# A mixture-of-experts kernel: activation, extra rows and steps of a round rearranged

## The chip, the core and the metric

One NeuronCore of a Trainium2 chip runs the whole block: input layer norm, one projection, two kinds of mixers, output projection, router, 32 experts with four chosen for each token, and the last layer norm. The metric is the device time of one execution in microseconds. TensorE does matmuls into PSUM, VectorE and ScalarE work on PSUM and SBUF, POOL (GpSimd) issues the indirect DMAs that gather and scatter token rows, and SyncE's queue (SP) issues the loads of the weights.

## The reference, cut to what matters

1024 tokens of width 1024; each goes to 4 of 32 experts, with a gate for each. The change lies in the expert part and behind it:

```python
hid = xb @ w1[e] + b1[e]                                  # 128 rows x 2048
x_glu = jnp.minimum(hid[..., ::2], 7.0)
x_lin = jnp.clip(hid[..., 1::2], -7.0, 7.0)
act = x_glu * jax.nn.sigmoid(1.702 * x_glu) * (x_lin + 1)
out = act @ w2[e] + b2[e]                                 # times the gate, summed over each token's experts
h = layer_norm(DEEPNORM_ALPHA * h + ffn)                  # the last layer norm
```

## The kernel before

**Rounds.** The experts are worked off in 32 rounds. Round r does `up` of expert r (8 blocks, k = 0 to 7, of 128 rows of w1) and then `down` of expert r-1 (4 blocks, b = 0 to 3, of w2). Each block of weights is 128x2048 float32, 1 MB. `weights` (L1174) loads it as `raw` (SyncE, a ring of RB = 6 buffers), has ScalarE round it to `wh` (L1185) and VectorE take the rest `wl` (L1188); these two are issued three blocks ahead (AH). TensorE then multiplies three times, wh by the high part of the operand, wl by the high part, wh by the low part: 12 matmuls of 512 columns for a block (L1213 in `up`, L1271 in `down`).

**Extra rows.** An expert takes 128 tokens, and the 18 fullest take 32 more (NH = 18, CX = 32). The 32 extra rows are multiplied in plain float32 with `raw`, in four column groups of TensorE beside each other, one group for each 512 columns: `extra` in `up` (L1206) and in `down` (L1261). Before, `extra` was called for two blocks at a time (XB = 2), behind the blocks 1, 3, 5 and 7 of `up` and 1 and 3 of `down`. A `raw` buffer is free once ScalarE, VectorE and, with extra rows, `extra` have read it.

**Steps.** Behind each block the loop calls `step(s)`, s = 0 to 7 for `up` and 8 to 11 for `down`, and this issues whatever `plan` has put there. So the order on every engine is fixed by these numbers:
- MP = 6: `begin2(r+2)`, the mark `oh` of which token goes to which slot (VectorE, L1139).
- SLP = -4, that is step 8 of the round before: `third`, which calls `slots`: TensorE turns the mark into token numbers (L1014, for extra rows also L1020), VectorE copies them (`st` L1029, `sv` L1004), computes the index, and POOL gathers the rows `xg`. For extra rows one step later (SLE): L1026, a small transposition, and another gather, `xe`.
- XP: the gathered rows are transposed (`front`), two pieces of `xg` at steps 4 and 5 and `xe` (L1165) at step 7.
- DP = 8 and 9: the two halves of the activation (`swiglu`, L1222); the extra rows' part runs directly behind `up`.
- TP: the activation is transposed, two pieces (L1150, then `ah` on ScalarE and `al` on VectorE, L1153) at steps 11 and 13 (step 1 of the next round), and that of the extra rows (L1248) at 14 (step 2).

All transpositions and slots share one bank of PSUM, tag `tr`: each waits until VectorE and ScalarE have read the one before. `up` writes four banks (`h`), `down` two (`o`), the extra rows one (`ex`).

**The end.** Behind round 31 two transpositions of the last expert's mark go into `kept`, the tokens' sums `ya_d` are loaded again into four ring buffers (`sums`, L1410), and `down` of the last expert leaves its result in SBUF. A loop over overflow blocks (L1417) makes no pass with these inputs. Then `final_norm` adds the last expert's rows by a matmul with the mark, and normalises eight tiles in groups of 3, 3 and 2 (FG): statistics on VectorE, and for each group a chain of small VectorE operations for the inverse root (`chain`). `advance` issues one step of the chain at each call; when the chain is done `finish` scales on ScalarE, adds on POOL and stores.

The parts ahead of the experts are ordered by the framework's scheduler, the experts and the final norm by hand (`manual_schedule`).

Of the kernel before, what the change touches and what calls it, by code (L numbers as in the profile page):

```python
# [8 lines left out]
FT = mybir.dt.float32  # L9
# [9 lines left out]
P = 128  # L19
# [24 lines left out]
FIRST = 10  # L44
XP = (4, 5, 7)
TP = (11, 13, 14)
SLP = -4
SLE = 1
# [5 lines left out]

XB = 2
FG = (0, 3, 6, 8)
# [10 lines left out]
SWI = 1.702  # L67
LIMIT = 7.0


# [730 lines left out]
def post_mix(tc, A, L):  # L801
# [60 lines left out]
    def half():  # L862
        for t in range(NT):
            n = slice(t * P, (t + 1) * P)
            y = p3.tile([P, 512], FT, name="y", tag="h1", bufs=H1B)
            sp.dma_start(y, y_d[n, 0:512])
            h = p3.tile([P, D], FT, name="h", bufs=UB)
            sp.dma_start(h, h_d[n, :])
            m = turn(lambda j: y[:, j * P:(j + 1) * P])
            for c in range(2):  # L870
                q, ps = product(*m, wa, c)
                ve.scalar_tensor_tensor(h[:, q], h[:, q], ALPHA, ps, op0=OP.mult, op1=OP.add)
            sp.dma_start(u_d[n, :], h)
        L["wb"] = [load_wo(4 + k) for k in range(4)]
        for nm, src, sh in (("lw", bcast(A["ln1_w"], D), [P, D]), ("lb", bcast(A["ln1_b"], D), [P, D]),
                            ("rb", bcast(A["router_b"], NE), [P, NE])):
            L[nm] = p3.tile(sh, FT, name="p3" + nm)
            sp.dma_start(L[nm], src)

        raw = p3.tile([96, D], FT, name="b2r", tag="wor", bufs=2)  # L880
        for i in range(3):
            sp.dma_start(raw[32 * i:32 * i + 32], A["b2"])
        L["b2"] = p3.tile([96, D], FR, name="b2s")
        ac.copy(L["b2"], raw)
        ve.tensor_tensor(L["b2"][64:96], raw[64:96], f32(L["b2"])[64:96], op=OP.subtract)

        bh = L["bh"]
        for i in range(2):
            q = slice(i * FF, (i + 1) * FF)
            b1 = p3.tile([96, FF], FT, name="b1", tag="wor", bufs=2)  # L890
            for g in range(3):
                sp.dma_start(b1[32 * g:32 * g + 32], A["b1"][:, q])
            ac.copy(bh[:, q], b1)
            for n in (64, 32):
                ve.tensor_tensor(b1[:n], b1[:n], bh[:n, q], op=OP.subtract)
                ac.copy(bh[:n, q], b1[:n])
        L["rwt"] = p3.tile([P, KD + 3, NE], FT, name="rwt")
        gp.memset(L["rwt"][:, KD:], 0.0)
        sp.dma_start(L["rwt"][:, :KD], A["router_w"])
# [214 lines left out]
def experts(tc, A, L):  # L1114
# [3 lines left out]
    with ExitStack() as cx:  # L1118
# [54 lines left out]

        def weights(j, ahead):  # L1174

            while len(raws) < min(j + src[1], len(stream)):
                raw = wr.tile([P, 2 * FF], FT, name="raw", tag=src[0], bufs=src[2])
                sp.dma_start(raw, stream[len(raws)]())
                raws.append(raw)
            while len(ready) < min(j + 1 + ahead, len(stream)):  # L1180
                i = len(ready)
# [10 lines left out]
        def up(j0, sel, xh, xl, xt, step=lambda s: None):  # L1192
# [5 lines left out]

            def extra(k, raw):
                if px is None:  # L1200
                    return
                if k == 0:
# [4 lines left out]

            late = []
            for k in range(KD):
                raw, h, l = weights(j0 + k, AH[xt is not None] if src[0] == "raw" else 0)  # L1210
                for x, w, z in ((xh, h, False), (xh, l, False), (xl, h, k == KD - 1)):
                    for c, m in enumerate(cols):
                        pe.matmul(ps[:, c], x[:, k], w[:, m], start=False, stop=z)  # L1213
                late.append((k, raw))
                if len(late) == XB:
                    for b in late:
                        extra(*b)
                    late.clear()
                step(k)
            return ps, px  # L1220

        def swiglu(glu, lin, g, l, sg):  # L1222
            ve.tensor_scalar(g, glu, LIMIT, None, op0=OP.min)  # L1223
            ac.activation(sg, g, AF.Sigmoid, scale=SWI)  # L1224
            ve.tensor_scalar(l, lin, LIMIT, -LIMIT, op0=OP.min, op1=OP.max)
            ve.scalar_tensor_tensor(l, l, 1.0, g, op0=OP.add, op1=OP.mult)
            ve.tensor_tensor(l, l, sg, op=OP.mult)

# [23 lines left out]
        def down(j0, ah, al, ax, gate, idx, step=lambda s: None, o=None):  # L1252
            po = pq.tile([P, 2, 512], FT, name="o")
            px = pq.tile([P, 512], FT, name="ex") if ax is not None else None

            def extra(b, raw):
                for c in range(2 if px is not None else 0):
                    for kk in range(2):
# [3 lines left out]

            late = []
            for b in range(4):
                raw, h, l = weights(j0 + b, AH[ax is not None] if src[0] == "raw" else 0)
                for kk in range(2):
                    k = 2 * b + kk
                    for x, w, z in ((ah, h, False), (ah, l, False), (al, h, k == KD - 1)):
                        for c in range(2):
                            m = slice(1024 * kk + 512 * c, 1024 * kk + 512 * c + 512)  # L1270
                            pe.matmul(po[:, c], x[:, k], w[:, m], start=(k == 0 and x is ah and w is h), stop=z)  # L1271
                late.append((b, raw))
                if len(late) == XB:
                    for x in late:
                        extra(*x)
                    late.clear()
                step(KD + b)
# [58 lines left out]
        def step(r, s):  # L1336
            for f in jobs.pop(12 * r + s, ()):
                f()

        at = {}  # L1340
        for r in range(NE + 1):
# [6 lines left out]
        with tc.manual_schedule():  # L1348
# [11 lines left out]
            for r in range(NE):  # L1360
# [17 lines left out]
                parts, turns, a = act(*hid)  # L1378
                run_all(parts[:-2])
                for i in range(2):  # L1380
                    jobs.setdefault(12 * r + DP + i, []).insert(0, parts[i - 2])
                for w, f in zip(TP, turns):
                    plan(r, w, f)
# [8 lines left out]
            for s in range(KD):  # L1392
                step(NE, s)

            ring = lambda: wr.tile([P, 2 * FF], FT, name="raw", bufs=RB)
            kept = ring()
            oht = kept[:, :S].rearrange("p (t q) -> p t q", t=NT)
            for g in range(2):
                ps = pq.tile([P, 4, P], FT, name="tr")
                for j in range(4):  # L1400
                    pe.matmul(ps[:, j], last_oh[0][:, 4 * g + j], idb, start=True, stop=True)
                ac.copy(oht[:, 4 * g:4 * g + 4], ps)
            wb = ring().rearrange("p (i d) -> p i d", i=2)
# [4 lines left out]
            def sums():  # L1408
                for g, y in enumerate(ys):
                    sp.dma_start(y, ya_d[2 * g * P:2 * (g + 1) * P, :].rearrange("(t p) d -> p t d", p=P))  # L1410
            sums()
            down(at["d", NE - 1], *prev, o=kept[:, S:])
            pq_.__exit__(None, None, None)
# [36 lines left out]
def final_norm(tc, A, L, ep, pt, wb, ys, oht, o):  # L1450
# [50 lines left out]

    def advance(to_end=False):
        nonlocal run
        while run is not None:
            if next(run[0], run) is run:
                finish(*run[1:])
                run = None
            if not to_end:
                return

    for g0, g1 in zip(FG, FG[1:]):
        for t in range(g0, g1):
# [7 lines left out]
            advance()  # L1520
        advance(True)
        run = (chain(g0, g1), g0, g1)
        next(run[0])
    bp.append(pt.tile([P, 2, 512], FT, name="y", bufs=3))
    for c in range(2):
        pe.matmul(bp[0][:, c], L["ons"][0:1], wb[0:1, 1, 512 * c:512 * c + 512], start=True, stop=True)
    advance(True)

# [57 lines left out]
```

## Time and profile before

| what | value |
|---|---|
| median of 3 runs | 2582.07 us (2574.61 to 2583.59) |
| profiled execution | 2580.89 us, span 2579.2 us, granted TensorE clock 0.972 |
| TensorE (PE) busy | 2399.2 us, 93% |
| VectorE (DVE) busy | 1928.0 us, 75% |
| ScalarE (ACT) busy | 1321.3 us, 51% |
| POOL busy | 400.6 us, 16% |
| moved by DMA | 606.63 MB, mean 235 GB/s |

The shares are means over the whole span. The first 40% of it are the mixers and the router; the rounds of the experts begin at about 1035 us and the final norm at 2531.76 us. A group of instructions is named by the line of the kernel, the engine and the tiles (out<-in). A timeline row merges equal instructions that follow each other (x4 is four), and its duration reaches to the end of the last, which overlaps the start of the next group: the distance of two starts is what a group costs TensorE. In brackets is the idle time ahead of it and what ended it. PEclk is the granted clock as a share of full speed.

### The profile page before, as it was taken

Reading aid. Unit: us, or ns where it says so; the run is one execution under the profiler, and the core shown is the slowest. Engines: PE = TensorE matmul, PEld = TensorE weight load, DVE = VectorE, ACT = ScalarE, POOL = GpSimd, SP = SyncE. Lnnn points to the kernel's source line nnn. Section 1 sums busy time; section 2 is a strip of 40 time slices with the busy share of each in tenths; the row PEclk is TensorE's granted clock in tenths of the full one; section 3 lists DMA queues with packets and bytes.
Section 4 is the critical chain, followed back from the end, with each engine's and each line's share of the span. In section 5 each row is a group of like instructions: output and inputs, shape, how many; then the busy total and the mean of one; then the engine's idle time right before and its main releaser. Section 6 shows DMA issues by size and latency. Waiting matters only on the chain. (4 is left out here: it accounts for less than half of the span.)

```text
span 2579.2 us, 37473 instructions
## 1 busy us (share of the span) xinstructions
PE 2399.2 (93%) x14105; PEld 1808.3 (70%) x14105; DVE 1928.0 (75%) x2886; ACT 1321.3 (51%) x1610; POOL 400.6 (16%) x370
## 2 busy tenths in 40 slices
PE   5999998989988996899999999999999999999986
PEld 5778998977776674657666666766676666667663
DVE  8367334376887687779788888888888888888884
ACT  3254432354344432456666656666565655666661
POOL 4400211123122011011101011011110110111012
PEclk9999999999999997899999999999999999999998
DMA  6323864228446424768878778888877897788973
GB/s 228 130 74 136 284 203 86 69 70 259 158 150 242 138 83 180 258 206 308 299 301 322 274 294 301 311 292 322 297 282 284 312 330 282 277 298 306 344 279 136
DMA packets 184442, 606.63 MB, mean 235 GB/s; under 512 B 69881, under 2 KB 95609, under 8 KB 130626
## 3 DMA queue, kind: packets, MB, share of 16 engines
q1 hardware_dynamic: 155810, 525.24, 55.0%
q0 software_dynamic: 17456, 65.02, 8.9%
q10 hardware_dynamic: 10992, 13.93, 1.8%
q8 instruction: 113, 1.85, 0.3%
q14 instruction: 71, 0.58, 0.1%
HBM read 518.64 MB, written 85.50 MB: 234 GB/s over the span
## 5 line engine op out<-in xcount | busy, mean ns | idle before, releaser
L1188 DVE TENSOR_TENSOR wl<-raw,wh 128x2048 fp32r<-128x2048 f32 x384 | 873.8, 2289 | 195.2 <-ACT wh L1185 194.1
L1185 ACT CAST wh<-raw 128x2048 fp32r<-128x2048 f32 x381 | 720.6, 1906 | 110.6 <-DMA raw<-w 83.4
L1213 PE MATMUL h<-wh,xh 128*128 128x512 f32 x1024 | 299.6, 414 | 0.9 <-ACT wh L1185 0.9
L1213 PE MATMUL h<-wl,xh 128*128 128x512 f32 x1024 | 281.3, 396 | 1.1 <-DVE wl L1188 1.1
L1213 PE MATMUL h<-wh,xl 128*128 128x512 f32 x1024 | 280.3, 395 | 0.0
L1213 PEld LDWEIGHTS h<-wl,xh 128*128 128x128 f32 x1024 | 193.2, 189 | 48.2 <-DVE wl L1188 1.6
L1213 PEld LDWEIGHTS h<-wh,xl 128*128 128x128 f32 x1024 | 192.4, 188 | 46.6
L1213 PEld LDWEIGHTS h<-wh,xh 128*128 128x128 f32 x1024 | 184.3, 190 | 52.9 <-ACT wh L1185 10.6
L1009 POOL DMA_INDIRECT xg<-h_d,idx x32 | 71.6, 2239 | 924.0 <-PE slots L1026 469.5
L153 PE MATMUL mm<-whi,hT_lo 128*128 128x256 f32 x640 | 187.1, 293 | 10.9 <-DVE hT_lo L182 7.3
L151 PE MATMUL mm<-whi,hT_hi 128*128 128x256 f32 x640 | 187.4, 294 | 6.0 <-ACT sq L476 4.3
L152 PE MATMUL mm<-wlo,hT_hi 128*128 128x256 f32 x640 | 186.1, 292 | 0.0
L1271 PE MATMUL o<-wh,ah 128*128 128x512 f32 x512 | 173.3, 420 | 0.0
L1271 PE MATMUL o<-wl,ah 128*128 128x512 f32 x512 | 164.9, 404 | 0.0
L1271 PE MATMUL o<-wh,al 128*128 128x512 f32 x512 | 164.0, 402 | 0.0
L1224 ACT ACTIVATE sm<-gm 128x512 f32<-128x512 f32 x64 | 40.4, 632 | 211.9 <-DVE gm L1223 211.9
L1206 PE MATMUL ex<-raw,xt 128*32 128x512 f32 x1152 | 139.7, 603 | 0.0
L153 PEld LDWEIGHTS mm<-whi,hT_lo 128*128 128x128 f32 x640 | 126.9, 199 | 12.9 <-DVE hT_lo L182 8.5
L151 PEld LDWEIGHTS mm<-whi,hT_hi 128*128 128x128 f32 x640 | 126.9, 198 | 9.3 <-ACT sq L476 4.7
L152 PEld LDWEIGHTS mm<-wlo,hT_hi 128*128 128x128 f32 x640 | 126.9, 198 | 0.0
L1271 PEld LDWEIGHTS o<-wh,ah 128*128 128x128 f32 x512 | 92.1, 193 | 34.8 <-issue 15.1
L1271 PEld LDWEIGHTS o<-wl,ah 128*128 128x128 f32 x512 | 98.8, 193 | 24.1
(432 smaller groups left out, 4177.7 us busy)
## 6 DMA issues: line engine op xcount, KB each, us to landing
raw<-w SPq DMA_DIRECT2D x384, 1024.0 KB
pks<-pk_d SPq DMA_DIRECT2D x16, 1152.0 KB
pk_d<-pk POOLq DMA_DIRECT2D x16, 896.0 KB, 5.6
h_d<-h SPq DMA_DIRECT2D x17, 512.0 KB
raw<-w_fx ACTq DMA_DIRECT2D x8, 1024.0 KB
fx_d<-fraw POOLq DMA_DIRECT2D x64, 128.0 KB, 2.6
qkvo<-fx_d SPq DMA_DIRECT2D x32, 256.0 KB
x<-x SPq DMA_DIRECT2D x8, 512.0 KB
```

Source lines behind the costliest of these rows:

```text
L151: pe.matmul(ps, hi[:, k, n], whi[:, k], start=(k == 0), stop=False)
L152: pe.matmul(ps, hi[:, k, n], wlo[:, k], start=False, stop=False)
L153: pe.matmul(ps, lo[:, k, n], whi[:, k], start=False, stop=(k == KD - 1))
L1009: gp.indirect_dma_start(out=x, out_offset=None, in_=h1_d, in_offset=bass.IndirectOffsetOnAxis(ap=idx[0:m, i:i + 1], axis=0))
L1185: ac.copy(highs[i], raw)
L1188: ve.tensor_tensor(l, raw, f32(h), op=OP.subtract)
L1206: pe.matmul(px[32 * c:32 * c + 32], xt[:, k], raw[:, m], start=False, stop=(k == KD - 1))
L1213: pe.matmul(ps[:, c], x[:, k], w[:, m], start=False, stop=z)
L1224: ac.activation(sg, g, AF.Sigmoid, scale=SWI)
L1271: pe.matmul(po[:, c], x[:, k], w[:, m], start=(k == 0 and x is ah and w is h), stop=z)
```

## The change

- **Activation.** `b1`'s linear half gets 1.0 added before it is split into `bh`, so that PSUM holds x_lin + 1. The sigmoid reads the unclipped gate from PSUM; the limit is applied to the product x * sigmoid(1.702 x), at the value TOP which this has at 7. VectorE's operations per half go from four to three.
- **Extra rows.** `extra` runs for four blocks at a time, behind block 1 (blocks 0 to 3) and block 5 (blocks 4 to 7) of `up`, and behind block 1 of `down` (blocks 0 to 3).
- **Steps.** SLP goes from -4 to -5 (slots at step 7, L1026's at step 8), XP's third from 7 to 6, TP's third from 14 to 15.
- **End.** In the last round both halves run directly behind `up`, the two transpositions of the mark go to steps 8 and 9 of it, and those of the activation to steps 10 and 11.
- **Final norm.** `advance` issues two steps of the chain at each call.

```diff
-XP = (4, 5, 7)
-TP = (11, 13, 14)
-SLP = -4
+XP = (4, 5, 6)
+TP = (11, 13, 15)
+SLP = -5
-XB = 2
+XB = 4
+XM = 1
+TOP = LIMIT / (1.0 + math.exp(-SWI * LIMIT))
...
+            lin = b1.rearrange("p (c g f) -> p c g f", g=2, f=256)[:, :, 1]
+            ve.tensor_scalar(lin, lin, 1.0, None, op0=OP.add)
             ac.copy(bh[:, q], b1)
...
-        def weights(j, ahead):
-            while len(raws) < min(j + src[1], len(stream)):
+        def load(n):
+            while len(raws) < min(n, len(stream)):
                 raw = wr.tile([P, 2 * FF], FT, name="raw", tag=src[0], bufs=src[2])
                 sp.dma_start(raw, stream[len(raws)]())
                 raws.append(raw)
+        def weights(j, ahead):
+            load(j + src[1])
...
-                late.append((k, raw))
-                if len(late) == XB:
-                    for b in late:
-                        extra(*b)
-                    late.clear()
+                if px is not None and k % XB == XM:
+                    for b in range(k - XM, k - XM + XB):
+                        extra(b)
                 step(k)
...
-            ve.tensor_scalar(g, glu, LIMIT, None, op0=OP.min)
-            ac.activation(sg, g, AF.Sigmoid, scale=SWI)
-            ve.tensor_scalar(l, lin, LIMIT, -LIMIT, op0=OP.min, op1=OP.max)
-            ve.scalar_tensor_tensor(l, l, 1.0, g, op0=OP.add, op1=OP.mult)
-            ve.tensor_tensor(l, l, sg, op=OP.mult)
+            ac.activation(sg, glu, AF.Sigmoid, scale=SWI)
+            ve.tensor_scalar(l, lin, 1.0 + LIMIT, 1.0 - LIMIT, op0=OP.min, op1=OP.max)
+            ve.tensor_tensor(g, glu, sg, op=OP.mult)
+            ve.scalar_tensor_tensor(l, g, TOP, l, op0=OP.min, op1=OP.mult)
...
-                late.append((b, raw))
-                if len(late) == XB:
-                    for x in late:
-                        extra(*x)
-                    late.clear()
+                if px is not None and b == XM:
+                    for x in range(XB):
+                        extra(x)
                 step(KD + b)
...
+        def turn_oh(g):
+            ps = pq.tile([P, 4, P], FT, name="tr")
+            for j in range(4):
+                pe.matmul(ps[:, j], last_oh[0][:, 4 * g + j], idb, start=True, stop=True)
+            if g == 0:
+                load(len(stream))
+                kept.append(ring())
+            ac.copy(kept[0][:, :S].rearrange("p (t q) -> p t q", t=NT)[:, 4 * g:4 * g + 4], ps)
...
-                run_all(parts[:-2])
-                for i in range(2):
-                    jobs.setdefault(12 * r + DP + i, []).insert(0, parts[i - 2])
-                for w, f in zip(TP, turns):
+                if r < NE - 1:
+                    run_all(parts[:-2])
+                    for i in range(2):
+                        jobs.setdefault(12 * r + DP + i, []).insert(0, parts[i - 2])
+                else:
+                    run_all(parts)
+                    for g in range(2):
+                        plan(r, KD + g, lambda g=g: turn_oh(g))
+                for w, f in zip(TP if r < NE - 1 else (10, 11), turns):
                     plan(r, w, f)
...
-    def advance(to_end=False):
+    def advance(n=2):
         nonlocal run
         while run is not None:
             if next(run[0], run) is run:
                 finish(*run[1:])
                 run = None
-            if not to_end:
+            n -= 1
+            if n == 0:
                 return
```

## Rows read from the trace of the kernel before

**Rows 1.** Windows, 1150 to 2500 us: us, busy of each engine, PEclk, DMA share, GB/s.

```profile
1150.00:2500.00 1350.00, 1318.57 (x7040) 920.65 (x7039) 1136.55 (x1070) 832.55 (x669) 165.97 (x90) 0.99 0.82 303
```

**Rows 2.** Waits of TensorE, 1150 to 2540 us: who waited for whom: total, times, longest.

```profile
PE slots L1026 <- DVE sv L1004: 19.8, 11, 3.7
PE tr L1248 <- DVE al L1153: 11.0, 7, 1.8
PE tr L1150 <- DVE al L1153: 6.6, 2, 6.3
PE y L1466 <- ACTq L1417: 2.2, 1, 2.2
```

**Rows 3.** Timeline of TensorE at the longest L1026 wait: start us, us, line, operation.

```profile
2100.92 0.36 PE L1026 MATMUL slots<-ident,st 6*128 6x6 f32 x2 [3.71 <-DVE sv L1004]
...
2102.22 1.05 PE L1271 MATMUL o<-wl,ah 128*128 128x512 f32 x2
2103.08 1.05 PE L1271 MATMUL o<-wh,al 128*128 128x512 f32 x2
```

**Rows 4.** Timeline of VectorE ahead of the same wait.

```profile
2097.71 0.69 DVE L1223 TENSOR_SCALAR gm<-h 128x512 f32<-128x512 f32 x1
...
2100.63 0.14 DVE L1004 COPY sv<-slots 128x6 f32<-128x6 f32 x1
```

**Rows 5.** Windows of 10 us in which the granted clock is below 1.

```profile
1170.00:1180.00 10.00, 7.54 (x27) 5.71 (x27) 9.58 (x21) 4.18 (x4) 3.27 (x2) 0.83 0.99 393
...
2330.00:2340.00 10.00, 7.70 (x28) 6.18 (x29) 9.20 (x20) 5.99 (x5) 3.25 (x2) 0.83 0.97 390
2510.00:2520.00 10.00, 6.23 (x22) 4.93 (x23) 3.83 (x4) 4.51 (x5) 2.38 (x1) 0.54 0.53 100
```

**Rows 6.** Waits of ScalarE, 1150 to 2500 us.

```profile
ACT sm L1224 <- DVE gm L1223: 194.2, 59, 4.3
...
ACT wh L1185 <- DMA raw<-w: 72.1, 54, 3.0
```

**Rows 7.** Timeline of TensorE around one run of the extra rows.

```profile
1468.70 1.09 PE L1213 MATMUL h<-wh,xl 128*128 128x512 f32 x4
1469.73 1.92 PE L1206 MATMUL ex<-raw,xt 128*32 128x512 f32 x16
1471.58 1.20 PE L1213 MATMUL h<-wh,xh 128*128 128x512 f32 x4
1472.61 1.10 PE L1213 MATMUL h<-wl,xh 128*128 128x512 f32 x4
```

**Rows 8.** The page's group of the extra rows' matmuls in `up`.

```profile
L1206 PE MATMUL ex<-raw,xt 128*32 128x512 f32 x1152 | 139.7, 603 | 0.0
```

**Rows 9.** Timeline of TensorE, second half of an `up` with extra rows.

```profile
1157.26 0.66 PE L1150 MATMUL tr<-ident,xg 128*128 128x128 f32 x4
...
1163.45 1.92 PE L1206 MATMUL ex<-raw,xt 128*32 128x512 f32 x16
```

**Rows 10.** Timeline of VectorE, the same stretch.

```profile
1160.38 2.29 DVE L1188 TENSOR_TENSOR wl<-raw,wh 128x2048 fp32r<-128x2048 f32 x1 [1.11 <-ACT wh L1185]
1162.59 1.49 DVE L1139 TENSOR_TENSOR oh<-ioc,pv 128x1280 bf16<-128x1280 bf16 x1
```

**Rows 11.** Waits of SyncE's queue, 2500 us to the end.

```profile
SPq L1417 <- SPq L1417: 8.2, 4, 2.6
```

**Rows 12.** Timeline of ScalarE behind the second last expert.

```profile
2504.63 3.68 ACT L1185 CAST wh<-raw 128x2048 fp32r<-128x2048 f32 x2
...
2508.70 1.12 ACT L1281 ACTIVATE o<-o,gate 128x1024 f32<-128x1024 f32 x1
```

**Rows 13.** Timeline of VectorE, last tile of the final norm.

```profile
2561.18 1.28 DVE L1519 SCALAR_TENSOR_TENSOR raw<-y,fmv,raw 128x1024 f32<-128x1024 f32 x1
```

**Rows 14.** Timeline of ScalarE, the final norm's second group.

```profile
2563.03 3.23 ACT L1496 ACTIVATE raw<-raw,frr 128x1024 f32<-128x1024 f32 x3 [5.62 <-DVE frr L1487]
```

**Rows 15.** Timeline of POOL, the same group.

```profile
2564.26 6.96 POOL L1497 TENSOR_TENSOR raw<-raw 128x1024 f32<-128x1024 f32 x3 [1.86 <-ACT raw L1496]
```

More of the change, by code (lines that the diff above doesn't have):

```diff
@@ L1197, in up, with extra @@
                 pe.matmul(ps[:, c], sel, bh[:, m], start=True, stop=False)
-            def extra(k, raw):
-                if px is None:
-                    return
+            def extra(k):
+                raw = raws[j0 + k]
                 if k == 0:
@@ L1206, in extra @@
                     pe.matmul(px[32 * c:32 * c + 32], xt[:, k], raw[:, m], start=False, stop=(k == KD - 1))
-            late = []
             for k in range(KD):
-                raw, h, l = weights(j0 + k, AH[xt is not None] if src[0] == "raw" else 0)
+                _, h, l = weights(j0 + k, AH[xt is not None] if src[0] == "raw" else 0)
                 for x, w, z in ((xh, h, False), (xh, l, False), (xl, h, k == KD - 1)):
@@ L1254, in down, with extra @@
             px = pq.tile([P, 512], FT, name="ex") if ax is not None else None
-            def extra(b, raw):
-                for c in range(2 if px is not None else 0):
+            def extra(b):
+                raw = raws[j0 + b]
+                for c in range(2):
                     for kk in range(2):
@@ L1261, in extra @@
                         pe.matmul(px[32 * g:32 * g + 32], ax[:, kk, 32 * b:32 * b + 32], raw[:, m], start=(b == 0), stop=(b == 3))
-            late = []
             for b in range(4):
-                raw, h, l = weights(j0 + b, AH[ax is not None] if src[0] == "raw" else 0)
+                _, h, l = weights(j0 + b, AH[ax is not None] if src[0] == "raw" else 0)
                 for kk in range(2):
@@ L1338, in step @@
                 f()
+        ring = lambda: wr.tile([P, 2 * FF], FT, name="raw", bufs=RB)
+        kept = []
+        def turn_oh(g):
[6 more added lines that the diff above has]
+            ac.copy(kept[0][:, :S].rearrange("p (t q) -> p t q", t=NT)[:, 4 * g:4 * g + 4], ps)
         at = {}
@@ L1393, in experts @@
                 step(NE, s)
[L1395 to L1402, printed above, removed]
             wb = ring().rearrange("p (i d) -> p i d", i=2)
@@ L1411, in experts @@
             sums()
+            kept = kept[0]
+            oht = kept[:, :S].rearrange("p (t q) -> p t q", t=NT)
             down(at["d", NE - 1], *prev, o=kept[:, S:])
@@ L1520, in final_norm @@
             advance()
-        advance(True)
+        advance(0)
         run = (chain(g0, g1), g0, g1)
@@ L1526, in final_norm @@
         pe.matmul(bp[0][:, c], L["ons"][0:1], wb[0:1, 1, 512 * c:512 * c + 512], start=True, stop=True)
-    advance(True)
+    advance(0)
 def L_lor(lor, which):
```

## The prediction

> **What bounds the kernel now.** I read the page's engine shares first, then the windows of the stretch in which the 32 experts run, then TensorE's waits there, then the timelines at the longest of them. From 1150 to 2500 us TensorE is busy 1318.57 of 1350 us, VectorE 1136.55, the DMA engines 0.82 of the time at 303 GB/s [rows 1]. So TensorE sets the pace of this stretch, and what counts is the 31 us in which it stands still and what it does less efficiently than it could.
>
> The 31 us have two names [rows 2]. For 19.8 us (11 times) it waits at L1026, the transposition of the extra rows' slot values, for VectorE's `sv` copy; for 11.0 us (7 times) at L1248, the transposition of the extra activations, for the `al` subtraction. The third row, 6.6 us, is almost all one wait of 6.3 us at the very end, and the fourth is already the 2.2 us ahead of the final norm. In the longest L1026 wait (3.71 us, [rows 3]) VectorE is not idle: from 2097.71 on it does the four operations of one half of the activation, and only then, at 2100.63, the `sv` copy [rows 4]. They stand ahead of it in program order, and TensorE has only one block (12 matmuls, 2.8 us by three groups of 0.93, [rows 7]) between L1020 and L1026.
>
> After such a wait the clock falls: pairs of matmuls of 512 columns, which at full clock start 0.47 us apart (groups of four 0.93, [rows 7]), start 0.86 us apart behind it [rows 3], which is the level of 1.2 in place of 2.4 GHz. In windows of 10 us, seven show a granted clock below 1 between 1150 and 2500; the first is 0.83 and the last 0.83 [rows 5], and summed over the seven, 10 us times what is missing is 8.5 us.
>
> **The change, part by part.** The profiled execution took 2580.89 us, 1.2 below the median of the three runs; the sum is made against it.
>
> 1. Slots one step earlier (SLP -5). L1014/L1020 and the copies of their result now follow the last block of `up`, ahead of the activation's halves; L1026 follows one block of `down` later. Between them VectorE has `st`, `sv` (0.14 us, [rows 4]) and four more as small, and no half. Counted from the end of block 5 of an `up` with extra rows, by the durations of part 4: `oh` ends at 10.4, the `wl` behind it at 12.6, the copies at 13.1 us; TensorE has done L1014 and L1020 at 11.0 and block 0 of `down` at 13.9. So the copies are 0.8 us ahead. The 19.8 us go, with 1 us left over (0 to 3): -18.8. The 8.5 us of half clock belong to these waits (each of the seven windows lies on or behind one): -8.5.
>
> 2. TP's third entry from 14 to 15: L1248 stands two blocks behind the `al` piece in place of one. Its waits were at most 1.8 us and a block is 2.8: -11.0. XP's third from 7 to 6 puts the `xe` transposition one block behind the second `x` piece. The two `x` pieces already stand one block apart, with the same work on ScalarE and VectorE, and no wait is listed for that ([rows 2] are TensorE's largest, the fourth 2.2 us): 0. If each of the 17 or so `xe` pieces waited as long as L1248 did on average where it waited, 1.6 us, that would be 27 us; nearest is the pair of `x` pieces, so 0.
>
> 3. Extra rows for four blocks at a time. An extra run of two blocks, alone between plain matmuls: the last plain group starts at 1468.70 and would be done at 1469.63 (groups start 0.93 apart); the run starts 1469.73, the next group 1471.58, and that one takes 1.03 [rows 7]. So 0.10 + 1.85 + 0.10. Its inside can be no shorter than 512 columns in four passes at 2.4 GHz, 0.85 us a block, 1.71 for two (the four column groups run beside each other, as 16 records in 1.85 us show); so up to 0.14 of it is start and drain. Two runs made one save 0.20 at the edges and 0 to 0.14 inside, 0.28 as I take it. The 1152 records of L1206 [rows 8] are 64 for each expert with extra rows, so 18 experts; each has two fewer runs in `up` and one fewer in `down`: 54 x 0.28 = 15 us. Against it: in the old plan transpositions stood directly behind a run and shared its edge ([rows 9] has one), and three a round no longer do; at half an edge each, 0.05 x 54 = 3 us. By 0.20 and a whole edge lost it is 5 us, by 0.34 and none lost 18; I take -12. What it needs early, the raw blocks two ahead, is already there: ScalarE casts three blocks ahead. The buffers of blocks 2, 3, 6 and 7 come free earlier, none later.
>
> 4. The wait this adds: L1014 needs the mark `oh` (L1139), which is issued at step 6, and now only one block lies between. Queued behind L1014 is all of TensorE's work. In one round with extra rows the transposition at step 5 is at 1157.26, the two blocks behind it end at 1163.4 (the run there moves away) [rows 9]; VectorE's `wl` runs 1160.38 to 1162.59 and `oh` then to 1163.99 [rows 10]. L1014 would stand ready at 1163.4 and wait 0.6 us. In rounds without extra rows the same working gives 0.2 to 0.3, and where `xe` adds 0.45 us of TensorE's time about 0.1. Over some 28 rounds that is 11 x 0.6 + 11 x 0.25 + 6 x 0.15 = 10 us. Bounds: 0, if VectorE runs ahead by its lighter queue; 25, if each wait of ScalarE for a raw block (72.1 us in 54 times, [rows 6]) that falls there is passed on. A wait of 0.6 us is a quarter of the shortest that I saw a fall of the clock behind, so no clock is charged. I take +10.
>
> 5. The activation itself. Per half 0.69 us of VectorE fall away (the first of the four, [rows 4]), and ScalarE's sigmoid no longer waits for it: 194.2 us of waiting, up to 4.3 each [rows 6], during which ScalarE's casts stood behind it. TensorE waits for neither of the two in the middle of the stretch, so this is worth 0 directly; it keeps part 4's wait small. If the waits for a late `wl` behind the halves show up later in another form, B prices it. The two added passes on `b1` are of 96x512: at most 0.69 each by the same row, some 1.4 if nothing hides them, 0 if something does: +1.
>
> 6. The end. The last round's halves come directly behind `up`, the one-hot transpositions go into the previous `down`, and the 6.3 us wait with its 9 us at half clock (window 0.54, [rows 5]) are gone: the last `down` ends about 11 us earlier. But the final norm cannot use this. SyncE waits at L1417, the loop that is left without a pass, for the four reloads of `ya_d` (8.2 us in four waits, [rows 11]); they can start only when the scatter of the second last expert has landed, and its `o` was scaled at 2508.70 [rows 12], because ScalarE had two casts (3.68 us) and one `ah` ahead of it. In the new order `o` comes 0.8 to 1.6 us earlier, so the norm starts 1.5 us earlier instead of 11. And then TensorE has stood still for 11 us instead of 2.2 [rows 2]: its first tiles run at half clock, at a loss of 2.5 to 4.5 us, taken as 3.5. In the norm two steps of the chain per call let the second group's `finish` begin before the last tile's 1.28 us pass and three chain steps, not behind them [rows 13, 14]; it starts at 2563.03 on ScalarE, and POOL's three additions from 2564.26 set the end [rows 15]: -2. Together 0, between -10 (the reloads don't hold the norm) and +5.
>
> **Sum.** -18.8 - 8.5 - 11.0 - 12 + 10 + 1 + 0 = -39.3, so 2541.6 on the profiled execution; with the 1.2 to the median, 2543.
>
> **Rivals.**
> A. *The new wait takes the place of the old.* For: `oh` stands behind a `wl` that stands behind a cast that can wait for its raw block; the margin is nil in part 4. Against: the two `x` pieces show VectorE in step with TensorE at that point of the round. If one more `wl` gets ahead, the wait is 0.6 + 2.29 = 2.9 us in 28 rounds, 81 us, and as 7 windows of 8.5 us came with 11 waits of this size, 22 us of clock: 2542 - 10 + 103 = 2635. It decides from (39 + 10)/28 = 1.75 us a round on. Slower: 6%.
> B. *The gain is lost on the way: the stream of weights.* At 303 GB/s and 0.82 of the DMA time a stretch 40 us shorter needs 0.845. Single windows show 393 GB/s [rows 5], so the mean allows it; but the raw blocks come through six buffers in bursts, and casts already wait 72.1 us for them. If half of the gain of parts 1 to 3 (25 us) turns into waits for `wh`: 2543 + 25 = 2568. 10%.
> C. *Both engines read the same PSUM bank.* In the new activation ScalarE's sigmoid and VectorE's clip read the two halves of one bank; before, the sigmoid read SBUF (`gm`). If they are kept apart, VectorE waits at each half for a cast under way (1.84 us, [rows 12]) and the sigmoid (by a pass of VectorE on the same tile 0.69), less the 0.69 saved: 1.8 x 60 = 110 us of VectorE, against 213 us in which it was idle [rows 1]. If a fifth of it reaches TensorE: 2543 + 22 = 2565. 6%. The Trainium skill, "PSUM — Partial Sum Buffer", section "PSUM bank collisions raise a hardware error", says of this that two engines must not access one bank in the same partitions at once, reads included, and that software has to keep them apart; no row of this trace shows such a pair, so by that rule C would be the case, by the trace alone it is open.
> D. *The end is worth its whole 11 us* (the reloads are not what the norm waits for): 2543 - 10 = 2533, inside the range. 10%.
>
> **Numbers.** Forecast as summed 68%, A 6, B 10, C 6, D 10. Range of the sum: best 0 for part 4, 18 for part 3 and 10 for the end gives 2517; worst 25, 4 and +5 gives 2571; I state 2518 to 2568. A measurement of this kernel can tell 0.5% from no change, 13 us, so 2569 and 2595 are the edges. Faster 0.84, same 0.10, slower 0.06.
>
> **What would show it.** Right: L1026 and L1248 gone from TensorE's waits; the windows at clock 1 throughout; L1206 in runs of 32 records starting twice per `up`; ScalarE's wait at the sigmoid small; a wait at L1014 for `oh` of some tenths of a us; the norm's first tiles at half clock behind an idle stretch of about 11 us. Wrong: waits at L1014 above 1.7 us, waits at L1213 for `wh` or `wl`, or a clip on VectorE that waits for the sigmoid.

## The result and the profile after

The changed kernel takes 2537.9 us against 2582.8 us before (medians; ratio 0.9823, 95% interval 0.9808 to 0.9838): 45 us faster, 5 us from the forecast of 2543. The profiled execution took 2537.4 us. The number came out; the runs below show that the way to it did not. The activation, priced at 0, carries the gain, and the slots' step, priced at -27, costs time without it.

The page's engine shares and the window of the expert stretch, after the change (the window answers to [rows 1]):

```profile
PE 2377.8 (94%) x14105; PEld 1810.4 (71%) x14105; DVE 1873.3 (74%) x2806; ACT 1323.9 (52%) x1610; POOL 406.8 (16%) x370
```

```profile
1150.00:2500.00 1350.00, 1330.20 (x7159) 944.46 (x7158) 1106.50 (x1014) 849.38 (x682) 175.79 (x91) 1.00 0.82 307
```

TensorE's waits from 1150 to 2540 us, which answer to [rows 2], and the two waits of ScalarE that answer to [rows 6]:

```profile
PE y L1479 <- SPq L1430: 9.8, 1, 9.8
PE slots L1019 <- DVE oh L1144: 7.1, 12, 0.6
PE o L1275 <- ACT o L1283: 1.7, 1, 1.7
PE tr L1155 <- DVE xl L1158: 0.8, 1, 0.8
```

```profile
ACT wh L1193 <- DMA raw<-w: 47.4, 16, 5.5
ACT sm L1228 <- DVE gm L1230: 46.8, 30, 2.2
```

The waits at L1026 and L1248 (L1031 and L1252 now) are gone, a wait of 0.6 us for `oh` has come in 12 rounds, every 10 us window from 1150 to 2480 shows a granted clock of 1.00, and the sigmoid's wait has fallen from 194.2 to 46.8 us. In kind all of this is as forecast (the wait for `oh` was forecast in some 28 rounds), and none of it tells which edit did it.

To compare runs I use the time from the first bias matmul of `up` in round 3 to that in round 31 ("rounds 3 to 30"): it leaves out the end, and the start, where round 2 alone lasts 56.4 us in the changed kernel and 53.4 in e7, which differs from it in the last round only. Before it is 1182.27 to 2469.93, 1287.7 us; after, 1181.62 to 2428.09, 1246.5 us: -41.2 of the 43.5 us by which the span fell. Each value is from one profiled execution; kernels with the same code in these rounds (after and e7; e8, e11 and e12) agree within 0.8 us.

| kernel | median us | ratio to before (95%) | rounds 3 to 30 | against after |
|---|---|---|---|---|
| before | 2582 to 2584 | 1 | 1287.7 | +41.2 |
| after | 2537.9 | 0.9823 (0.9808 to 0.9838) | 1246.5 | 0 |
| e1 old activation | 2592.3 | 1.0036 (1.0023 to 1.0048) | 1293.0 | +46.6 |
| e2 new activation alone | 2548.0 | 0.9857 (0.9835 to 0.9879) | 1260.2 | +13.8 |
| e3 slots a step back | 2548.6 | 0.9866 (0.9844 to 0.9888) | 1254.7 | +8.3 |
| e4 slots a step earlier alone | 2592.6 | 1.0036 (1.0021 to 1.0052) | 1301.0 | +54.6 |
| e5 extra rows in twos | 2535.5 | 0.9816 (0.9798 to 0.9834) | 1250.9 | +4.4 |
| e6 extra activations a step back | 2549.2 | 0.9874 (0.9853 to 0.9895) | 1260.7 | +14.2 |
| e7 last round back | 2534.0 | 0.9809 (0.9790 to 0.9828) | 1247.3 | +0.8 |
| e8 mark a step earlier | 2525.3 | 0.9779 (0.9761 to 0.9797) | 1237.8 | -8.7 |
| e9 four operations, sigmoid free | 2548.4 | 0.9863 (0.9845 to 0.9882) | 1253.8 | +7.4 |
| e10 three operations, sigmoid behind | 2587.8 | 1.0019 (1.0006 to 1.0032) | 1291.4 | +44.9 |
| e11 e7 and e8 together | 2521.1 | 0.9768 (0.9752 to 0.9783) | 1237.6 | -8.8 |
| e12 e11 and the table's stores moved | 2514.1 | 0.9729 (0.9714 to 0.9744) | 1237.3 | -9.2 |

### The profile page after: what moved, and what is told of

It reads as the page before. It is cut to its first block, busy times and chain, and to the rows that moved or that the text cites. A ratio compares the mean times of both kernels' runs of the same rounds, so it can differ in the third digit from the quotient of the medians.

```text
span 2535.7 us, 37299 instructions
## 1 busy us (share of the span) xinstructions
PE 2377.8 (94%) x14105; PEld 1810.4 (71%) x14105; DVE 1873.3 (74%) x2806; ACT 1323.9 (52%) x1610; POOL 406.8 (16%) x370
## 3 DMA queue, kind: packets, MB, share of 16 engines
q1 hardware_dynamic: 155810, 525.24, 54.6%
## 5 line engine op out<-in xcount | busy, mean ns | idle before, releaser
L1219 PEld LDWEIGHTS h<-wl,xh 128*128 128x128 f32 x1024 | 194.2, 190 | 47.8 <-DVE wl L1196 1.0
L1014 POOL DMA_INDIRECT xg<-h_d,idx x32 | 49.7, 1552 | 777.4 <-PE o L1275 680.5
L1275 PE MATMUL o<-wh,ah 128*128 128x512 f32 x512 | 167.5, 408 | 1.7 <-ACT o L1283 1.7
L1213 PE MATMUL ex<-raw,xt 128*32 128x512 f32 x1152 | 132.2, 600 | 0.0
L1275 PEld LDWEIGHTS o<-wh,al 128*128 128x128 f32 x512 | 96.2, 188 | 23.2
```

The source lines that it names most:

```text
L1014: gp.indirect_dma_start(out=x, out_offset=None, in_=h1_d, in_offset=bass.IndirectOffsetOnAxis(ap=idx[0:m, i:i + 1], axis=0))
L1213: pe.matmul(px[32 * c:32 * c + 32], xt[:, k], raw[:, m], start=False, stop=(k == KD - 1))
```

## Experiments: which edit carries the gain

**e1**, the changed kernel with the old activation.

```diff
-ac.activation(sg, glu, AF.Sigmoid, scale=SWI)
+ve.tensor_scalar(g, glu, LIMIT, None, op0=OP.min)
+ac.activation(sg, g, AF.Sigmoid, scale=SWI)
...  (the clip, stt and product of before; b1 without the added one)
```

> The changed kernel with the four VectorE operations of the old activation and without the added one in b1. Theory (the activation is worth nothing by itself, since TensorE waits for neither engine there): 2537 us (2531 to 2546), ratio to the kernel before 0.980 to 0.986; VectorE busy some 43 us longer, ScalarE's wait at the sigmoid back above 150 us, TensorE's waits as in the changed kernel to 3 us. Rival 1 (the shorter activation is what keeps VectorE in step): half of its 41 us comes back, 2558 us, as waits at L1252 or L1155 for al. Rival 2 (in the new form ScalarE and VectorE take turns at one PSUM tile and TensorE pays for it): faster, 2525 us.

It took 2592 us: all other edits together, without the activation, are slower than the kernel before. Theory and both rivals missed; rival 1 had the direction and was 34 us short. In TensorE's waits, 1150 to 2500 us, the largest row is the bias of the next `up`, which waits for VectorE to have read `h`:

```profile
PE h L1203 <- DVE lm L1227: 23.5, 12, 2.3
```

With 8.8 us of waits for `al` and `xl` and 11.9 us lost by a granted clock below 1 this makes about 44 of the 46.6 us.

**e2**, the kernel before with the new activation alone (the `swiglu` and the `b1` lines of the change).

> The kernel before with the new activation alone (three operations, the added one in b1). Theory: the half that stands ahead of the sv copy is at most 0.69 us shorter, so the 19.8 us of waits at the transposition of the slot values shrink by up to 11 x 0.69 = 7.6 us, and b1 adds about 1: 2577 us (2572 to 2584). Rival 1 (the activation carries a third of the gain): 2565 us or less. Rival 2 (taking turns at the PSUM tile costs): 2590 us or more, as longer waits for sv and al.

It took 2548 us: 35 of the 45 us. Rival 1's number holds (2565 us or less); its third of the gain was too small. So the activation is worth 35 us alone and 54 beside the other edits. TensorE's waits, 1150 to 2500 us:

```profile
PE tr L1252 <- DVE al L1157: 6.9, 5, 1.4
PE tr L1154 <- DVE al L1157: 3.8, 1, 3.8
PE slots L1030 <- DVE sv L1008: 2.6, 6, 0.4
```

The 19.8 us at the slot values [rows 2] are down to 2.6 with the transposition where it always was: the long waits of 2.5 to 3.7 us are 0.44 each, far more than 0.69 less, and the granted clock is 1.00 in every window up to 2480 us. ScalarE and VectorE ahead of a usual one of them show where 2.03 us went, first in the kernel before (wait of 2.47 us at 1405.70), then in e2 (0.44 us at 1402.65):

```profile
1398.03 0.42 ACT L1224 ACTIVATE sx<-gx 128x256 f32<-128x256 f32 x1 [3.32 <-DVE gx L1223]
...
1400.28 2.29 DVE L1188 TENSOR_TENSOR wl<-raw,wh 128x2048 fp32r<-128x2048 f32 x1 [0.96 <-ACT wh L1185]
```

```profile
1395.79 0.39 ACT L1228 ACTIVATE sx<-ex 128x256 f32<-128x256 f32 x1 [2.09 <-PE ex L1210]
...
1398.02 2.29 DVE L1192 TENSOR_TENSOR wl<-raw,wh 128x2048 fp32r<-128x2048 f32 x1 [0.25 <-ACT wh L1189]
```

From the extra rows' first operation on VectorE to this `wl` it is 2.70 us before and 1.46 in e2: 0.71 of the difference is idle time ahead of `wl`, whose cast stands behind the sigmoid, the other 0.53 the operation and VectorE's wait for the sigmoid. The half behind it, ahead of the `sv` copy, takes 2.73 and 1.93 us. So at this wait the operation that is gone and the freed sigmoid both count.

**e4**, the kernel before with the slots a step earlier, nothing else.

```diff
-SLP = -4
+SLP = -5
```

> The kernel before with SLP -5 alone. Theory (terms 1 and 4 of the sum: 19.8 and 8.5 us go, 3 at the restarts, 7.7 come as waits for oh): 2583 - 24 = 2559 us (2553 to 2567), with all windows between 1150 and 2500 at clock 1. Rival (without the shorter activation the new wait for oh is as long as the old one was): 2575 us or more.

It took 2593 us, 10 slower than before, where I had expected 24 faster. That is in the rival's range, but not by the rival's wait: there is no row for `oh`. The same view:

```profile
PE tr L1248 <- DVE al L1153: 23.3, 12, 2.4
PE h L1197 <- DVE lm L1225: 8.1, 12, 1.4
PE slots L1014 <- ACT xt L1166: 7.3, 16, 0.5
PE tr L1150 <- DVE al L1153: 2.6, 7, 0.4
```

L1026 is gone, and 41 us stand elsewhere. VectorE's stretch behind `up` was not made shorter, only put in another order: the slots' copies go first, the halves end later, and whatever reads them next waits, L1248 for twice as long as in [rows 2], and L1197, the bias of the next `up`, which can't overwrite `h` before VectorE has read it. L1014 also waits for the `xt` copy, since XP's third step is still 7: the edit that I priced at 0 belongs to this one.

**e3**, the other way round: the changed kernel with SLP -4.

> The changed kernel with SLP back at -4, all else as changed. Theory: the waits for sv come back (19.8 us less 11 x 0.69 = 12 us), with half clock behind them (about 7 us) and the start-up of TensorE behind each stall (2), while the waits for oh go (-7.7): 2551 us (2544 to 2562). Rival (with the shorter activation the copy is in time wherever it stands): only the waits for oh go, 2530 us.

As the theory said, 2549 us; the row is

```profile
PE slots L1031 <- DVE sv L1009: 12.8, 6, 2.1
```

Beside all the other edits the step is worth 8.3 us in rounds 3 to 30, where by itself it cost 13.4. (In these rounds the copies' waits of 10.7 us and 6.9 us of clock, less 6.4 us of waits for `oh`, would make 11; the rest of the account is open.) In e2, where everything but the activation is old, the same copies cost TensorE only 2.6 us; which of the other edits makes 12.8 of it was not separated. Rows of a wait say what it amounts to; they don't say that moving the waiting instruction removes it.

## Experiments: what in the activation does it

Either there are fewer operations, or the sigmoid no longer stands behind VectorE. First the rows. Timeline of the second part of round 4 in e1 (start, duration, engine, line, operation; idle time before it in brackets; lines of TensorE's `down` left out):

```profile
1271.55 0.68 DVE L1225 TENSOR_SCALAR gm<-h 128x512 f32<-128x512 f32 x1
...
1272.27 0.63 ACT L1226 ACTIVATE sm<-gm 128x512 f32<-128x512 f32 x1 [2.96 <-DVE gm L1225]
1272.81 1.90 ACT L1191 CAST wh<-raw 128x2048 fp32r<-128x2048 f32 x1
...
1274.74 2.29 DVE L1194 TENSOR_TENSOR wl<-raw,wh 128x2048 fp32r<-128x2048 f32 x1 [0.38 <-ACT wh L1191]
...
1276.95 0.69 DVE L1225 TENSOR_SCALAR gm<-h 128x512 f32<-128x512 f32 x1
...
1278.29 1.04 PE L1203 MATMUL h<-bh,sel 96*128 96x512 bf16 x4 [2.14 <-DVE lm L1227]
```

The same place in the changed kernel:

```profile
1258.79 0.59 ACT L1228 ACTIVATE sm<-h 128x512 f32<-128x512 f32 x1
...
1260.07 1.92 ACT L1193 CAST wh<-raw 128x2048 fp32r<-128x2048 f32 x1 [0.69 <-PE o L1275]
...
1260.53 2.28 DVE L1196 TENSOR_TENSOR wl<-raw,wh 128x2048 fp32r<-128x2048 f32 x1
1262.74 0.68 DVE L1229 TENSOR_SCALAR lm<-h 128x512 f32<-128x512 f32 x1
...
1263.34 0.67 DVE L1230 TENSOR_TENSOR gm<-h,sm 128x512 f32<-128x512 f32 x1
...
1264.05 0.60 ACT L1228 ACTIVATE sm<-h 128x512 f32<-128x512 f32 x1 [2.06 <-DVE gm L1230]
1264.05 0.69 DVE L1231 SCALAR_TENSOR_TENSOR lm<-gm,lm 128x512 f32<-128x512 f32 x1
...
1264.65 2.28 DVE L1196 TENSOR_TENSOR wl<-raw,wh 128x2048 fp32r<-128x2048 f32 x1
1266.85 0.69 DVE L1229 TENSOR_SCALAR lm<-h 128x512 f32<-128x512 f32 x1
...
1268.71 1.03 PE L1205 MATMUL h<-bh,sel 96*128 96x512 bf16 x4
```

In the old form there is a ring over two engines. The sigmoid waits for the limit `gm`; the cast of the next block stands behind the sigmoid in ScalarE's order (ScalarE was idle for 2.96 us ahead of it); VectorE's `wl` needs that cast; and the next limit stands behind `wl`. From one half to the next: 0.72 + 0.54 + 1.93 + 2.21 = 5.40 us (1271.55 to 1276.95). In the new form the sigmoid of the first half (1258.79) has run before VectorE comes to that half, and the cast behind it (1260.07) before VectorE needs it. The sigmoid of the second half (1264.05) does wait for VectorE, for the first half's product, but the cast that the next `wl` needs is already done. So VectorE is never idle here, and the period is 0.60 + 0.71 + 0.60 + 2.20 = 4.11 us. TensorE's bias then starts without a wait, against 2.14 us of waiting in e1.

**e9** keeps the sigmoid free and adds a fourth operation.

```diff
 ve.tensor_scalar(l, lin, 1.0 + LIMIT, 1.0 - LIMIT, op0=OP.min, op1=OP.max)
+ve.tensor_scalar(l, l, 1.0 + LIMIT, 1.0 - LIMIT, op0=OP.min, op1=OP.max)
```

> The changed kernel with a fourth VectorE operation of the old length in each part of the activation (the clip of the linear half, done once more on its own result), the sigmoid still reading PSUM at once. It tells the number of operations from the sigmoid's place. Theory (in the traces one half follows the other after 5.40 us in the old form and 4.11 in the new; 0.69 of that is the operation, 0.60 the stall in which VectorE's wl waits for a cast that stands behind the sigmoid): 4.80 us from half to half; the last read of h comes 0.41 + 2 x 0.69 = 1.8 us later than in the changed kernel, which has 0.6 to spare, so L1206 (the bias of the next up) waits 1.2 us where it waited 2.1 in e1: 2538 + 13 x 1.2 + 6 of clock = 2560 us (2550 to 2570). Rival 1 (the count of operations is all): as e1, 2592 us. Rival 2 (only the sigmoid's place counts): 2538 to 2545 us.

**e10** keeps three operations and puts the sigmoid behind the first; the linear half's lower clip is left out.

```diff
-ac.activation(sg, glu, AF.Sigmoid, scale=SWI)
-ve.tensor_scalar(l, lin, 1.0 + LIMIT, 1.0 - LIMIT, op0=OP.min, op1=OP.max)
-ve.tensor_tensor(g, glu, sg, op=OP.mult)
-ve.scalar_tensor_tensor(l, g, TOP, l, op0=OP.min, op1=OP.mult)
+ve.tensor_scalar(g, glu, LIMIT, None, op0=OP.min)
+ac.activation(sg, g, AF.Sigmoid, scale=SWI)
+ve.scalar_tensor_tensor(l, lin, 1.0 + LIMIT, g, op0=OP.min, op1=OP.mult)
+ve.tensor_tensor(l, l, sg, op=OP.mult)
```

> The changed kernel with three VectorE operations of which the first (the limit) stands ahead of the sigmoid as in the old form; the lower clip of the linear half is left out for that. Theory: the casts stand behind the sigmoid again, and with one operation in place of two between the limit and the last product, VectorE also waits about 0.3 us for the sigmoid in each part; the last read of h comes some 2 us later than in the changed kernel, L1206 waits about 1.3 us in 13 rounds: 2563 us (2550 to 2580). Rival 1 (the count is all): 2538 us. Rival 2 (the sigmoid's place is all): 2590 us.

(The bias of the next `up` stands at L1205 in both, not L1206.) Three operations with the sigmoid behind VectorE cost 2588 us, as good as nothing saved against e1's 2592; four with it free cost 2548, between the theory's range (2550 to 2570) and that of rival 2 (2538 to 2545). Timeline of e10 at the same place, then TensorE's wait at that bias in e10 and in e9, 1150 to 2500 us:

```profile
1269.21 0.68 DVE L1228 TENSOR_SCALAR gm<-h 128x512 f32<-128x512 f32 x1
...
1269.92 0.64 ACT L1229 ACTIVATE sm<-gm 128x512 f32<-128x512 f32 x1 [2.96 <-DVE gm L1228]
...
1270.46 1.90 ACT L1193 CAST wh<-raw 128x2048 fp32r<-128x2048 f32 x1
...
1272.39 2.29 DVE L1196 TENSOR_TENSOR wl<-raw,wh 128x2048 fp32r<-128x2048 f32 x1 [0.98 <-ACT wh L1193]
...
1274.60 0.68 DVE L1228 TENSOR_SCALAR gm<-h 128x512 f32<-128x512 f32 x1
```

```profile
PE h L1205 <- DVE lm L1230: 23.8, 12, 2.4
```

```profile
PE h L1205 <- DVE gm L1231: 7.1, 12, 0.7
```

The period of e10 is 5.39 us (1269.21 to 1274.60), that of the old form with four operations 5.40: the operation that was saved became idle time, 0.98 us in place of 0.38 ahead of `wl`, since the ring's length holds only the limit and none of the operations behind it. So the theory for e10 (2563) was wrong, and rival 2 (the sigmoid's place) right. In e9 the period is 4.59 (1266.58 to 1271.17), below the 4.80 expected, since the added operation is shorter than 0.69:

```profile
1267.30 0.43 DVE L1230 TENSOR_SCALAR lm<-lm 128x512 f32<-128x512 f32 x1
...
1271.17 0.68 DVE L1229 TENSOR_SCALAR lm<-h 128x512 f32<-128x512 f32 x1
```

It took 0.43 us, where the one that reads `h` in PSUM takes 0.68, and the period grew by 0.48 us: e9 holds about two thirds of a saved operation. Of the 47 us between e1 and the changed kernel in rounds 3 to 30, 39 come with the sigmoid's place (e1 to e9, +46.6 to +7.4) although e9 has four operations too; the last 7 with the operation (by an estimate, 7.4 x 0.69 / 0.48, some 11 for one of full length, which leaves 36 for the place). Taken in the other order the operation is worth 2 (e1 to e10): it pays only once the ring is open. This split holds beside the other edits. Beside the kernel before, the pair was not run; there the slots' copies lie between the two halves, and the rows of e2 show both at work.

## Experiments: the other steps

**e5**, the extra rows in twos again (XB 2, behind blocks 1, 3, 5, 7 of `up` and 1, 3 of `down`).

> The changed kernel with the extra rows for two blocks at a time again (XB 2: behind blocks 1, 3, 5, 7 of up and 1, 3 of down). Theory: 54 more runs at 0.19 to 0.28 us an edge give +10 to +15, less what transpositions share with an edge: 2538 + 10 = 2548 us (2543 to 2555). Rival 1 (the merged runs save no time inside, and the gain of the rounds came from the waits): 2538 us. Rival 2 (the longer runs make what follows late): faster in twos, 2533 us.

By the times, no difference that these runs can tell (0.9816 against 0.9823): the theory's 2548 missed, and the 2536 us lie between the two rivals. By rounds 3 to 30 the fours save 4.4 us, and the rounds show two terms. Where no other wait changes, a merged run saves what the sum said: round 4, 45.49 us in twos and 44.93 in fours, two merges, 0.28 each; round 8, 42.44 and 42.15, one merge, 0.29. The 49 merges of these rounds come to 14 us. But in twos TensorE's waits have no row at all for `oh`: the run that used to stand between block 7 and L1019 gave VectorE its time. In fours eleven of the waits lie in these rounds, 6.4 us (ten of 0.61, one of 0.34), and a round that has one loses some 0.2 us more than the wait; round 6, where the fours wait 0.8 us for `xl`, loses 1.0. That makes the 4.4.

**e8**, the mark `oh` one step earlier.

```diff
-MP = 6
+MP = 5
```

> The changed kernel with the mark oh one step earlier (MP 5 in place of 6). Theory: the 13 waits at L1019 for oh, 7.7 us, go, and nothing takes their place: 2538 - 8 = 2530 us (2527 to 2535). Rival 1 (oh ahead of the next wl makes that wl or xl late; its 1.4 us shows as waits at L1219 or L1155 in about 28 rounds): 2545 us. Rival 2 (VectorE is just in step and the wait moves to sv): 2538 us.

All 7.7 us of waits for `oh` went (13 with the one in round 0), and nothing came in their place: -8.7 in rounds 3 to 30 for the 6.4 us of waits that lay there. The time, 2525 us, is below the theory's range; the rest of the difference, 4.7 us, lies ahead of round 3, where the changed kernel's round 2 is 3 us longer than that of e7 with the same code.

**e6**, TP's third entry back at 14.

> The changed kernel with the third entry of TP back at 14. Theory: the waits at L1252 for al come back, 11.0 us in 7, and some 0.4 us at each restart: 2538 + 13 = 2551 us (2545 to 2556). Rival (the activation's second half is 0.69 us earlier by its shorter form, so the wait of 1.8 shrinks to 1.1 or less): 2538 + 7 = 2545 us or less. The trace tells them apart: 1.8 us a wait or 1.1.

As the theory said, 2549 us, +14.2 in rounds 3 to 30:

```profile
PE tr L1252 <- DVE al L1158: 11.1, 12, 2.2
```

Most waits are of 0.47 or 1.39 us, not 1.8 (the halves are earlier by the new activation, as the rival had it), but there are twelve in place of seven.

**e7**, the edits of the last round undone.

```diff
-if r < NE - 1:
...  (its body stays, for every round)
-else:
-    run_all(parts)
-    for g in range(2):
-        plan(r, KD + g, lambda g=g: turn_oh(g))
-for w, f in zip(TP if r < NE - 1 else (10, 11), turns):
+for w, f in zip(TP, turns):
...  (behind round 31)
+for g in range(2):
+    turn_oh(g)
```

> The changed kernel with the edits of the last round undone (halves, transpositions and one-hot matrix in their old places). Theory (the norm cannot start before the second last expert's rows have landed and been read back): the 6.3 us wait of TensorE comes back and the norm starts at most 1.5 us later, but on a TensorE that was not idle for 10 us just before it (2 us back): 2538 us (2535 to 2542). Rival (the end is worth its 11 us): 2549 us.

2534 us, 4 less than with the edits, 1 below the theory's range; the intervals overlap, but the end shows it: from the bias of round 31 to the last instruction, 103.85 us against 107.59. TensorE and then ScalarE around the end of the changed kernel:

```profile
2488.22 3.78 PE L1479 MATMUL y<-raw,ident 128*128 128x512 f32 x4 [9.77 <-SPq L1430]
2491.80 2.45 PE L1482 MATMUL y<-raw 128*128 128x512 f32 x4
2494.09 1.88 PE L1479 MATMUL y<-raw,ident 128*128 128x512 f32 x4
```

```profile
2465.80 1.12 ACT L1283 ACTIVATE o<-o,gate 128x1024 f32<-128x1024 f32 x1
```

and of e7:

```profile
2487.17 1.99 PE L1476 MATMUL y<-raw,ident 128*128 128x512 f32 x4 [2.69 <-SPq L1427]
2488.99 1.88 PE L1479 MATMUL y<-raw 128*128 128x512 f32 x4
2490.71 1.88 PE L1476 MATMUL y<-raw,ident 128*128 128x512 f32 x4
```

```profile
2464.46 1.12 ACT L1283 ACTIVATE o<-o,gate 128x1024 f32<-128x1024 f32 x1
```

Counted from the bias of round 31 (2428.09 and 2428.45), `o` of the second last expert is scaled at 37.7 us in the changed kernel and at 36.0 in e7: the added casts and copies stand ahead of it on ScalarE. The norm, which waits for that expert's rows, starts at 60.1 and 58.7. After 9.77 us of standing still the first three groups of the norm's matmuls start 3.58 and 2.29 us apart, after 2.69 us of it 1.82 and 1.72: that is the 2.3 us by which the norm itself is longer.

**e11** (e7's and e8's edits together) **and e12**, which also moves two stores:

```diff
-sp.dma_start(L["tab_d"], tab)
+gp.dma_start(L["tab_d"], tab)
...
-sp.dma_start(L["tabi_d"], tabi)
+gp.dma_start(L["tabi_d"], tabi)
```

> The changed kernel with the mark oh at step 5 and the edits of the last round undone. Theory (the two differences of e7 and e8 add up, -3.8 and -12.7): 2521 us (2517 to 2526). Rival (they share a part, start-up included): 2525 us or more.

> As the run before it, and the two stores of the table of left-over blocks issued from GpSimd's queue in place of SyncE's. Theory (SyncE stands for 16 us at the table's first store with the loads of the raw blocks queued behind it, and round 2 pays for it: casts wait 10.8 us for a block, TensorE 4.1 + 0.3 + 2.0 us with 5 us at half clock): 6 us less than the run before it, 2515 us (2511 to 2520). Rival (the loads wait for free buffers anyway): no difference, 2521 us.

2521.1 and 2514.1 us: both theories hold. SyncE's queue in e11 and in e12, 1080 to 1150 us:

```profile
1085.18 12.95 SPq L1182 DMA_DIRECT2D raw<-w  x4
1115.59 0.34 SPq L1111 DMA_DIRECT2D tab_d<-tab  x1
...
1116.67 2.33 SPq L1182 DMA_DIRECT2D raw<-w  x4
```

```profile
1087.59 33.09 SPq L1182 DMA_DIRECT2D raw<-w  x8
```

and the wait of SyncE's queue in e11 that names the table (`le`, of which VectorE works it out):

```profile
SPq L1426 <- DVE le L1100: 15.7, 1, 15.7
```

In e11 no raw block is asked for between 1098 and 1116 us, since the store of a table that VectorE is still working on stands ahead in the queue; in e12 the loads go on, and round 2 lasts 45.0 us in place of 52.6. e12 beats both kernels: ratio 0.9729 to the one before.

## Why the number came out, step by step

1. Slots a step earlier, -18.8 and -8.5. The step that failed: "The 19.8 us go". Alone the edit makes the kernel 10 us slower (e4). The counting of VectorE's queue at L1026 was right for that instruction, but the halves that are pushed behind were not followed to L1197 and L1248. Both sums, the waits and the half clock, went in this change; e2 shows that the activation alone takes nearly all of them.
2. TP, -11.0: right, 14.2 (e6). XP, 0: no run takes it out alone; e4, which has the slots' step without it, waits 7.3 us for `xt`.
3. Extra rows in fours, -12: right in size, 0.28 to 0.30 a merge and 14 us for the 49 merges of rounds 3 to 30 (e5); of the 3 us set against it nothing shows there.
4. The wait for `oh`, +10: right, 7.1 us, and its 0.6 us exactly; the rounds that I gave 0.1 to 0.25 have none but one of 0.34. It takes both the fours and the slots' step: neither e5 (twos) nor e3 (slots a step back) has it.
5. The activation, 0: wrong by 35 us alone and 54 in place. "TensorE waits for neither of the two" holds for the sigmoid and the limit, but both of TensorE's large waits were for the end of a VectorE stretch that the old activation made longer: in the kernel before by 1.24 us in the extra rows' part and 0.80 in the half ahead of `sv` (e2), and beside the other edits by 1.3 us in a half, 5.40 in place of 4.11, through the ring (e1). The rows were there: 194.2 us of the sigmoid's wait [rows 6], with casts behind it, and the `wl` that waits for its cast [rows 10]. I wrote that the shorter half only "keeps part 4's wait small". The +1 for the added pass on `b1` was not measured by itself.
6. The end, 0: -1.7 from the bias of round 31 up to the norm's start (forecast -1.5) and none behind it, where half clock (forecast +3.5) and the steps of the chain (-2) cancel. The -1.7 is luck: e7, without the edits of the last round, has -3.1, so these edits cost 1.4 there. In e7 the norm takes 45.1 us against 47.4 both before and after, so the chain is worth 2.3 and the clock costs 2.3; the last round's edits as a whole cost 3.7.

So it is luck that the sum of -39.3 met the trace's -43.5: two terms stood in each other's place, the -27.3 of the slots, which cost 10 alone, and the 0 of the activation, which is worth 35 alone. Rival A (a wait in the place of the old one) is what the slots' step does when it is alone. Its price for the clock counts eleven waits of one size; five of them are of 0.6 us, and behind those no window fell below 1. Rival C's order is there in part: in all 32 rounds the second half's sigmoid starts 0.03 to 0.04 us behind the end of the first half's product on VectorE, and no read of one tile by the one engine overlaps one by the other; the only overlaps are five of 0.02 to 0.04 us between `sm<-h` and `lx<-ex`, two tiles. This agrees with the Trainium skill, "PSUM — Partial Sum Buffer", section "PSUM bank collisions raise a hardware error", by which software has to keep two engines off one bank. But the two halves lie in different banks of `h` and share the tile `sm`, so these rows don't tell for which of them the sigmoid is held back. Its price is nil: no wait of the clip for the sigmoid is among VectorE's waits, and VectorE is not idle in the changed kernel's rows above. Rival B's loss did not come: waits of casts for raw blocks fell from 72.1 to 47.4 us. Rival D fell: TensorE stood still for 9.77 us instead.

What stays open: in round 2 the changed kernel is 3 us longer than e7, whose code is the same there. The windows from 1130 to 1150 us show it in the clock (0.66 and 0.83 against 0.85 and 0.98, 3.4 us), around a wait of TensorE for a cast (4.1 us against 2.8); why that wait differs is not shown.

## What to carry to other kernels

When the bounding engine waits for the end of another engine's stretch, take that stretch apart before pricing a reorder: follow each idle gap in it through the engines until the path closes, for a ring over two in-order queues has a length that an operation saved off the ring doesn't change, and one moved dependence does. Moving the waiting instruction alone hands the lateness to the next reader. And a sum that comes out is no proof of its terms: take the edits out one at a time, each alone and each from the whole.

## What the runs showed of the hardware

- A VectorE tensor_scalar on 128x512 f32 took 0.68 us with its source in PSUM and 0.43 with source and result in SBUF (e9).
- Behind a wait of 2.14 us TensorE's groups of four matmuls ran at 1.76 us from start to start in e1's round 5 in place of 0.93, the 1.2 GHz level; the ten windows of e1 below full clock between 1150 and 2480 us sum to 11.9 us, with waits of 1.8 to 2.3 us 12 times; in e9, with 12 waits of at most 0.7 us, all windows from 1150 to 2470 us show 1.00. Not every such wait is followed by a fall: behind e1's of 2.14 us at 1744.25 and the one of 2.47 us at 1405.70 in the kernel before, the windows stay at 1.00.
- Two runs of the extra rows (column groups, plain float32) made one saved 0.28 to 0.30 us a merge, start to start (e5).
- A store that waited 15.7 us for its data at the head of SyncE's queue kept the loads behind it from being asked for (e11); issued from GpSimd's queue, it left round 2 7.6 us shorter (e12).
